# Queries and keys of heads 1 to 3 of the second layer as seven products of halves

## The chip, the cores and the metric

The kernel runs on one core of one Trainium2 chip. A core has a matrix engine (TensorE, PE in the profile), a vector engine (VectorE, DVE), a scalar engine (ScalarE, ACT), GpSimd (POOL) and SyncE (SP), which issues most of the transfers. Each engine takes its instructions strictly in the order of its own queue and waits at the head of it until the semaphores that an instruction names have been reached. Weights of PE are loaded by instructions of their own, which the profile lists as PEld. The metric is the time of one execution on the device in microseconds, the median of several executions.

## What is computed

Two pre-norm residual layers and a final norm over 512 tokens of 1024 channels, in float32. The first layer (latent attention and pooling) is not touched. The second is a retention layer of four heads. Cut to what matters:

```python
h = rms_norm(x, norm_g)
q, k, v, gate = jnp.split(h @ w_in, [1024, 2048, 4096], axis=-1)
q = apply_rope(q.reshape(B, T, 4, 256), cos_r, sin_r)
k = apply_rope(k.reshape(B, T, 4, 256), cos_r, sin_r) * 256 ** -0.5
o = retention forward + retention backward, per head   # scores q k^T times a decay, times v
o = (o - mean(o)) * rsqrt(var(o) + eps) * gn_g         # per head and token
x = x + (o * silu(gate)) @ w_out
out = rms_norm(x, final_norm_g)
```

For each head the queries and the keys are products of the 512 x 1024 activations with 1024 x 256 weights: 256 columns of queries and 256 of keys.

## The kernel before

**Split numbers.** [...] ACT casts the high part, DVE subtracts it from the source to get the low part, and a product is then three matmuls: high by high, high by low, low by high (`mm3`, lines 71 to 76). Activations are kept split in SBUF (`hT`). Weights come from DRAM into a buffer `raw` of 128 x 1024 floats (four of them), are split into `wH` (four buffers) and `wL` (three), and are used then. So every weight tile costs a load, an ACT cast of 128 x 1024 and a DVE subtraction of 128 x 1024 before the first, or the third, matmul that uses it.

**Order.** All instructions are put into the engines' queues ahead of time by a scheduling layer that follows its own costs, so the order in the queues is not that of the source; instructions under `pin` keep the program's order. The order is fixed when the program is built.

**A head of the second layer** (loop at line 983) makes its queries and keys (`qk_gemm`, `rope_pair`), then, from head 1 on, the output projection of the head before (`r_out`: 8 groups of 12 matmuls, each added into the residual by DVE, line 925), then the scores (`r_scores`), the values and gates (`vg`) and the head's output (`r_head_out`). The last 4 transposes of `r_head_out` (`turn(3)`, line 877) are kept in `pend[2]` and put behind the first group of the next head's queries. The column sums that scale the output (`out_scale`) need the squares that ACT makes of the last product, and a power on POOL (line 177).

**Queries and keys before.** Four groups per head, each 128 columns by 512 tokens, with 24 matmuls of 512 columns: 96 matmuls. Four weight tiles are loaded and split. `rope_pair` then takes two groups at a time: four multiplications of 512, one subtraction, one addition, and two splits.

**Values and gates** (`vg`, line 776) already use another scheme: tokens are halved (first and last 256), the contraction is halved (even and odd blocks of 128 channels), and the two column halves are the gates and the values. Seven products of halves then take the place of eight (the scheme of Strassen and Winograd). The sums of halves of the activations (S1 to S4) are made once per layer (`sums_of_halves`, line 704) and kept split in `forms`; those of the weights are made per head, partly by transfers that POOL issues and that add in flight (`accum_op`, line 684), partly by DVE (lines 829, 839). There the seven products run as matmuls of 512 columns. The sums of weights lie in two buffers `tw`.

Of the kernel before, what the change touches and what calls it, by code (L numbers as in the profile page):

```python
# [12 lines left out]
F32R = mybir.dt.float32r  # L13
# [3 lines left out]
ALU = mybir.AluOpType  # L17
# [20 lines left out]
def trunk(ctx: ExitStack, tc: tile.TileContext, x, positions, a_norm_g, a_w_in, a_q_norm_g, a_w_uq,  # L38
# [29 lines left out]
    def f(ap):  # L68
        return ap.bitcast(F32)
# [55 lines left out]
    fsum = C("fsum", (P, 16))  # L125
    r2, nr2, r2s = [C(n, (P, 8))[:, 0:4] for n in ("r2", "nr2", "r2s")]
    C("fill", (P, 16))
    w_in = a_w_in[0]
# [211 lines left out]
    V.tensor_reduce(out=ss, in_=ssq.rearrange("p (t q) -> p t q", q=4), axis=AX.X, op=ALU.add)  # L340
    R = C("R", (P, T))
    rp = bcast(pow_mhalf(ss, 1.0 / DM))
# [423 lines left out]
    def rope_pair(pts, tag):  # L766
# [7 lines left out]
        return split(a, tag), split(c, tag)  # L774

    def vg(h, tt=None):

# [38 lines left out]
        if tt is None:  # L816
            tt = first_sums(h)
        product("A11", "X", b11, True)
# [36 lines left out]

    def r_scores(q, k, ds, tag):
        ss = []
        for j in range(4):
            tk = slice(j * P, (j + 1) * P)
            pt = PS("sc")  # L860
            for i in range(2):
                mm3(pt, k[i][0][:, tk], k[i][1][:, tk], q[i][0], q[i][1], i == 0, i == 1)
            s = S("t")
            V.scalar_tensor_tensor(out=s, in0=pt, scalar=r2s[:, j:j + 1], in1=ds[j], op0=ALU.mult, op1=ALU.mult)
            ss.append(split(s, tag))
        return ss

    def r_head_out(ss, vv, gs, tag):


        ys = []
        sq = S("sm", (P, 4))

        def turn(t):
            pt = PS("tr")
            for m in range(4):
                nc.tensor.transpose(pt[:, m * P:(m + 1) * P], gs[t][:, m * P:(m + 1) * P], ident)
            ys.append(split(pt, tag))

        for t in range(4):  # L880
            tk = slice(t * P, (t + 1) * P)
            pt = PS("mm")
            for j in range(4):
                mm3(pt, ss[j][0][:, tk], ss[j][1][:, tk], vv[j][0], vv[j][1], j == 0, j == 3)
            V.tensor_mul(gs[t], pt, gs[t])  # L885
            act(S("t"), pt, AF.Square, scale=r2[:, t:t + 1], accum_out=sq[:, t:t + 1])
            if t:
                turn(t - 1)
        return ys, sq, lambda: turn(3)

# [92 lines left out]
    for h in range(4):  # L983
        A, B = ("qk", "y") if h % 2 == 0 else ("y", "qk")
        if h == 0:
            res = [residual(0), residual(1)]
            next(res[0])
            pq = qk_gemm(0, 1)
            sums_of_halves(0)
            sums_of_halves(1)  # L990
            next(res[0])
            pq += qk_gemm(P, 1)
            pk = qk_gemm(1024, 1)
            sums_of_halves(2)
            sums_of_halves(3)
            next(res[1])
            next(res[1])
        else:
            pq = qk_gemm(h * 256, then=pend[2])
            pk = qk_gemm(1024 + h * 256, 1)  # L1000
            rs = out_scale(pend[1])
        q = rope_pair(pq, A)
        k = rope_pair(pk + qk_gemm(1024 + h * 256 + P, 1), A)
        if h == 0:
            V.tensor_add(ss2[:, 0:4], ss2[:, 0:4], ss2[:, 4:8])
            V.tensor_copy(r2, pow_mhalf(ss2[:, 0:4], 1.0 / DM))
            V.tensor_scalar(out=nr2, in0=r2, scalar1=-1.0, scalar2=1.0, op0=ALU.mult, op1=ALU.mult)
            V.tensor_scalar(out=r2s, in0=r2, scalar1=0.0625, scalar2=1.0, op0=ALU.mult, op1=ALU.mult)
        else:
            r_out(h - 1, pend[0], rs)  # L1010
        ss = r_scores(q, k, decay(h), B)
        vv, gs = vg(h, tt0 if h == 0 else None)
        pend = r_head_out(ss, vv, gs, A)
    for i in range(2):
# [48 lines left out]
```

## Time and profile before

| | |
|---|---|
| time, three runs | 794.54, 792.81, 792.67 us; median 792.81 |
| the profiled execution | 794.41 us, of which its span of instructions is 792.6 us |
| granted TensorE clock, mean | 0.998 |
| instructions | 9592 |
| data read from HBM, written | 76.87 MB, 2.10 MB |
| transfers, mean rate | 102 GB/s |

The rows of the profile name the engine, the source line, the tile that is written and those that are read, the shape and the count, then the time in which the engine was busy and the mean duration of one. Tile names are without buffer numbers there (`mm` is any buffer of that pool in PSUM). A row of the timeline gives the start in microseconds from the span's first instruction, and the duration; successive instructions of PE and DVE overlap, so the step from start to start is what one costs in a row of them.

### The profile page before, as it was taken

How to read it: one execution, taken by the hardware profiler on the slowest of the kernel's cores; microseconds unless marked ns; L12 is line 12 of the kernel's file. 1: busy time of each engine (PE TensorE's matmuls, PEld its weight loads, DVE VectorE, ACT ScalarE, POOL GpSimd, SP SyncE). 2: the span in 40 equal slices, each digit the busy share in tenths (PEclk: the TensorE clock that was granted, in tenths of full speed). 3: DMA queues.
4: the chain of work that ended last, by engine and by line, in shares of the span. 5: the costliest groups of instructions: out<-in, count | busy, mean ns of one | idle time of the engine just before them, and what ended most of it. 6: DMA issues, size and time to landing. Idle time of an engine off the chain costs nothing. (4 is left out here: it accounts for less than half of the span.)

```text
span 792.6 us, 9592 instructions
## 1 busy us (share of the span) xinstructions
PE 781.1 (99%) x3546; PEld 642.0 (81%) x3546; DVE 579.0 (73%) x938; ACT 403.4 (51%) x670; POOL 38.6 (5%) x60
## 2 busy tenths in 40 slices
PE   9999999999999999999999999999999999999996
PEld 7888888888888888888877888888888888888885
DVE  4689986768748677899679747787377884767845
ACT  6645346666626744318654832358333583334832
POOL 0010000000000000100010100100101001010003
PEclk9999999999999999999999999999999999999999
DMA  8722233132123312353315822447324373244202
GB/s 254 226 62 83 70 82 87 39 80 91 54 72 88 103 38 69 87 152 107 107 37 133 227 56 80 111 111 210 74 79 110 103 203 84 71 122 102 85 27 108
DMA packets 87832, 80.91 MB, mean 102 GB/s; under 512 B 7868, under 2 KB 67304, under 8 KB 87784
## 3 DMA queue, kind: packets, MB, share of 16 engines
q1 hardware_dynamic: 82984, 71.11, 29.8%
q0 software_dynamic: 4352, 8.39, 7.0%
q10 hardware_dynamic: 448, 0.79, 0.3%
q8 instruction: 28, 0.46, 0.2%
q14 instruction: 20, 0.16, 0.1%
HBM read 76.87 MB, written 2.10 MB: 100 GB/s over the span
## 5 line engine op out<-in xcount | busy, mean ns | idle before, releaser
L72 PE MATMUL mm<-hT,wH 128*128 128x512 f32 x352 | 139.0, 395 | 0.3 <-ACT wH L281 0.3
L75 PE MATMUL mm<-hT,wH 128*128 128x512 f32 x352 | 137.8, 392 | 0.0
L76 PE MATMUL mm<-hT,wL 128*128 128x512 f32 x352 | 137.8, 392 | 0.0
L108 ACT CAST wH<-raw 128x1024 fp32r<-128x1024 f32 (+3 forms) x77 | 70.7, 923 | 114.4 <-PE mm L75 91.3
L109 DVE TENSOR_TENSOR wL<-raw,wH 128x1024 fp32r<-128x1024 f32 (+3 forms) x77 | 81.4, 1059 | 13.1 <-issue 4.7
L72 PEld LDWEIGHTS mm<-hT,wH 128*128 128x128 f32 x352 | 66.5, 189 | 14.0 <-ACT wH L281 0.7
L76 PEld LDWEIGHTS mm<-hT,wL 128*128 128x128 f32 x352 | 66.5, 189 | 14.0 <-DVE wL L282 0.2
L75 PEld LDWEIGHTS mm<-hT,wH 128*128 128x128 f32 x352 | 66.5, 189 | 13.6
L784 ACT CAST wH<-raw 128x1024 fp32r<-128x1024 f32 x32 | 33.7, 1054 | 50.2 <-PE mm L76 20.2
L785 DVE TENSOR_TENSOR wL<-raw,wH 128x1024 fp32r<-128x1024 f32 x32 | 38.9, 1220 | 10.4 <-issue 7.2
L784 ACT CAST wH<-tw 128x1024 fp32r<-128x1024 f32 x24 | 25.1, 1047 | 40.9 <-PE mm L76 26.3
L904 ACT ACTIVATE wH<-raw,cols 128x512 fp32r<-128x512 f32 x32 | 21.4, 717 | 43.8 <-issue 32.8
L925 DVE SCALAR_TENSOR_TENSOR xT<-mm,sm,xT 128x512 f32<-128x512 f32 (+1 forms) x33 | 24.1, 731 | 25.1 <-PE mm L76 25.0
L75 PE MATMUL mm<-y,wH 128*128 128x512 f32 x96 | 37.2, 389 | 0.0
L76 PE MATMUL mm<-y,wL 128*128 128x512 f32 x96 | 37.2, 389 | 0.0
L72 PE MATMUL mm<-y,wH 128*128 128x512 f32 x96 | 37.2, 390 | 0.0
L785 DVE TENSOR_TENSOR wL<-tw,wH 128x1024 fp32r<-128x1024 f32 x24 | 29.3, 1220 | 2.8 <-PE tr L794 1.0
L794 PE MATMUL mm<-wL,hT 128*128 128x512 f32 x80 | 31.1, 389 | 0.0
L795 PE MATMUL mm<-wH,hT 128*128 128x512 f32 x80 | 31.1, 389 | 0.0
L792 PE MATMUL mm<-wH,hT 128*128 128x512 f32 x80 | 31.0, 389 | 0.0
L885 DVE TENSOR_TENSOR l<-mm,l 128x512 f32<-128x512 f32 x16 | 11.1, 692 | 23.9 <-PE mm L76 23.9
L504 DVE TENSOR_TENSOR xT<-mm,xT 128x512 f32<-128x512 f32 x24 | 16.4, 688 | 15.0 <-PE mm L76 14.8
(361 smaller groups left out, 1903.6 us busy)
## 6 DMA issues: line engine op xcount, KB each, us to landing
raw<-in_r_w_in_dram SPq DMA_DIRECT2D x48, 512.0 KB, 3.7
raw<-in_a_w_in_dram SPq DMA_DIRECT2D x25, 512.0 KB, 4.0
raw<-in_a_w_out_dram SPq DMA_DIRECT2D x16, 512.0 KB, 3.9
raw<-in_r_w_out_dram SPq DMA_DIRECT2D x16, 512.0 KB, 5.5
tw<-in_r_w_in_dram SPq DMA_DIRECT2D x8, 512.0 KB, 3.8
tw<-in_r_w_in_dram POOLq DMA_DIRECT2D x8, 512.0 KB, 6.6
raw<-in_r_w_in_dram POOLq DMA_DIRECT2D x8, 512.0 KB, 6.0
l<-in_x_dram SPq DMA_DIRECT2D x8, 256.0 KB, 4.7
```

Source lines behind the costliest of these rows:

```text
L72: i = mm(pt, lhsT=lH, rhs=rH, start=st, stop=False)
L75: mm(pt, lhsT=lH, rhs=rL, start=False, stop=False)
L76: mm(pt, lhsT=lL, rhs=rH, start=False, stop=sp)
L108: then(nc.scalar.copy(h[:, c], raw[:, c]))
L109: then(V.tensor_sub(l[:, c], raw[:, c], f(h[:, c])))
L784: nc.scalar.copy(wh, ws[i])
L785: V.tensor_sub(wl, ws[i], f(wh))
L792: mm(o, lhsT=lh, rhs=wh[:, c], start=first and i == 0 and k2 == 0, stop=False, skip_group_check=True)
L794: mm(o, lhsT=lh, rhs=wl[:, c], start=False, stop=False, skip_group_check=True)
L795: mm(o, lhsT=ll, rhs=wh[:, c], start=False, stop=last and k2 == 1, skip_group_check=True)
L904: act(wh[:, c], raw[:, c], AF.Copy, scale=g)
L925: V.scalar_tensor_tensor(out=a, in0=pt[:, :T // n], scalar=rs[:, t:t + 1], in1=a, op0=ALU.mult, op1=ALU.add)
```

## The change

For heads 1 to 3 the queries and keys are made together by `qk_halves`. It uses the halved activations and their sums that `vg` uses; the two column halves are now the queries and the keys of the head. Of the seven products each has 24 matmuls of 256 columns (4 blocks of the contraction, 2 halves of the 128 x 256 weight columns, 3 for the split): 168 in place of 96 of 512. The seven weight operands are: the plain blocks B11 (for A11), B21 (for A12) and B22 (for S4), the sum of two blocks made by an adding transfer for S1 (`tq`, loaded ahead by `qk_load` after the `vg` of the head before, into a buffer `tw`) and for S3 (`t3`), and, for S2 and A22, the first of these sums with B22, then B21, added by DVE.

Three PSUM tiles hold the sums: X (A11, then A12, the queries of the first 256 tokens), Z (S1, then S4) and Y (S2, then S3, then A22). Since the products accumulate in place, a tile is read by DVE between two products: Z after S1 (line 839 of the changed file), Y after S2 (line 846) and after S3 (line 851). The rotation (`rope`) is done for half of the tokens at a time: per call two multiplications of 512, a subtraction and an addition of 256, and two casts and two subtractions of 256 for the split, four calls per head. The keys come out with the opposite sign, which `nr2s` undoes in the scores of heads 1 to 3. The casts and the matmuls of S1 are told to be issued after the last multiplication by the gates and the last squares of the head before (`issue_after`).

Besides: the scale `R` of the first layer moves from a buffer of its own into one of the two `x2`, the buffer `fill` is halved, the scratch memory for the transfers that POOL issues is doubled to 2048 bytes, the first matmul of each head's scores is pinned, and the adding transfers for `vg` are pinned in all heads.

```diff
--- before.py
+++ after.py
@@ -123,8 +123,8 @@
     lg = C("lg", (P, 8))
     nlb = C("nlb", (P, 8))
     fsum = C("fsum", (P, 16))
-    r2, nr2, r2s = [C(n, (P, 8))[:, 0:4] for n in ("r2", "nr2", "r2s")]
-    C("fill", (P, 16))
+    r2, nr2, r2s, nr2s = [C(n, (P, 8))[:, 0:4] for n in ("r2", "nr2", "r2s", "nr2s")]
+    C("fill", (P, 8))
     w_in = a_w_in[0]
     G.memset(mhalf, -0.5)
     vrow0 = S("t")[:8, :P]
@@ -338,7 +338,7 @@
             act(junk[:, 0:256], xt[t][q], AF.Square, accum_out=ssq[:, 4 * t + q:4 * t + q + 1])
     ss = S("sm", (P, 4))
     V.tensor_reduce(out=ss, in_=ssq.rearrange("p (t q) -> p t q", q=4), axis=AX.X, op=ALU.add)
-    R = C("R", (P, T))
+    R = S("x2")
     rp = bcast(pow_mhalf(ss, 1.0 / DM))
     nc.scalar.copy(R, rp)
 
@@ -773,6 +773,90 @@
         V.tensor_add(c, c, d)
         return split(a, tag), split(c, tag)
 
+    def qk_load(tag, h, *srcs):
+        raw = S(tag, (P, 1024))
+        v = raw.rearrange("p (a b) -> p a b", a=4)
+        for i, (r, c) in enumerate(srcs):
+            one = wv[:, r, :, c * 1024 + h * 256:c * 1024 + (h + 1) * 256]
+            if i:
+                pin(G.dma_start(v, one, accum_op=ALU.add))
+            else:
+                nc.sync.dma_start(v, one)
+        return raw
+
+    def qk_halves(h, tag, tt, then, ends):
+
+
+        ps_ = {n: PS("mm") for n in "XZY"}
+
+        def load(tag, *srcs):
+            return qk_load(tag, h, *srcs)
+
+        def product(name, a, w, first):
+            wh, wl = S("wH", (P, 1024), F32R), S("wL", (P, 1024), F32R)
+            nc.scalar.copy(wh, w)
+            V.tensor_sub(wl, w, f(wh))
+            for u in range(2):
+                o = ps_[a][:, u * H2:(u + 1) * H2]
+                for k in range(4):
+                    c = slice(k * 256 + u * P, k * 256 + (u + 1) * P)
+                    rh, rl = forms[k][name]
+                    mm(o, lhsT=wh[:, c], rhs=rh, start=first and u == 0 and k == 0, stop=False,
+                       skip_group_check=True)
+                    mm(o, lhsT=wh[:, c], rhs=rl, start=False, stop=False, skip_group_check=True)
+                    mm(o, lhsT=wl[:, c], rhs=rh, start=False, stop=k == 3, skip_group_check=True)
+
+        X, Y, Z = (ps_[n] for n in "XYZ")
+        outs = {n: [(S(tag, dt=F32R), S(tag, dt=F32R)) for _ in range(2)] for n in "qk"}
+
+        def rope(n, half, c):
+
+            ts = slice(half * H2, (half + 1) * H2)
+            v = c.rearrange("p (u t) -> p u t", u=2)
+            m1, m2 = S("t"), S("t")
+            for m, tab in ((m1, cosr), (m2, sinr)):
+                V.tensor_mul(m.rearrange("p (u t) -> p u t", u=2), v,
+                             tab[:, ts].unsqueeze(1).to_broadcast([P, 2, H2]))
+            o = S("t")
+            V.tensor_sub(o[:, :H2], m1[:, :H2], m2[:, H2:])
+            V.tensor_add(o[:, H2:], m2[:, :H2], m1[:, H2:])
+            for u in range(2):
+                hh, ll = outs[n][u]
+                us = slice(u * H2, (u + 1) * H2)
+                nc.scalar.copy(hh[:, ts], o[:, us])
+                V.tensor_sub(ll[:, ts], o[:, us], f(hh[:, ts]))
+
+        b11 = load("raw", (0, 0))
+        product("A11", "X", b11, True)
+        p1 = S("t")
+        nc.scalar.copy(p1, X)
+        then()
+        b22 = load("raw", (1, 1))
+
+        with tc.issue_after(ends[0].ins), tc.issue_after(ends[1].ins):
+            product("S1", "Z", tt, True)
+        v = S("t")
+        V.tensor_add(v, Z, p1)
+        t3 = load("raw", (0, 1), (1, 1))
+        V.tensor_add(tt, tt, b22)
+        product("S4", "Z", b22, False)
+        b21 = load("raw", (1, 0))
+        product("S2", "Y", tt, True)
+        u2 = S("t")
+        V.tensor_add(u2, Y, p1)
+        V.tensor_add(u2, Z, u2)
+        rope("k", 0, u2)
+        V.tensor_add(tt, tt, b21)
+        product("S3", "Y", t3, False)
+        V.tensor_add(v, Y, v)
+        rope("k", 1, v)
+        product("A12", "X", b21, False)
+        rope("q", 0, X)
+        product("A22", "Y", tt, False)
+        V.tensor_add(p1, Y, p1)
+        rope("q", 1, p1)
+        return outs["q"], outs["k"]
+
     def vg(h, tt=None):
 
         tags = dict(X=("mm", "mm"), Z=("mm", "tr"), Y=("mm", "sc"))
@@ -814,7 +898,7 @@
 
         b11 = [load("raw", src(0, 0, i)) for i in rng]
         if tt is None:
-            tt = first_sums(h)
+            tt = first_sums(h, pin)
         product("A11", "X", b11, True)
         p1 = [S("t") for _ in rng]
         for p in rng:
@@ -853,15 +937,15 @@
             gs[2 + p] = c
         return vv, gs
 
-    def r_scores(q, k, ds, tag):
+    def r_scores(q, k, ds, tag, rs):
         ss = []
         for j in range(4):
             tk = slice(j * P, (j + 1) * P)
             pt = PS("sc")
             for i in range(2):
-                mm3(pt, k[i][0][:, tk], k[i][1][:, tk], q[i][0], q[i][1], i == 0, i == 1)
+                mm3(pt, k[i][0][:, tk], k[i][1][:, tk], q[i][0], q[i][1], i == 0, i == 1, i == 0 and j == 0)
             s = S("t")
-            V.scalar_tensor_tensor(out=s, in0=pt, scalar=r2s[:, j:j + 1], in1=ds[j], op0=ALU.mult, op1=ALU.mult)
+            V.scalar_tensor_tensor(out=s, in0=pt, scalar=rs[:, j:j + 1], in1=ds[j], op0=ALU.mult, op1=ALU.mult)
             ss.append(split(s, tag))
         return ss
 
@@ -882,11 +966,11 @@
             pt = PS("mm")
             for j in range(4):
                 mm3(pt, ss[j][0][:, tk], ss[j][1][:, tk], vv[j][0], vv[j][1], j == 0, j == 3)
-            V.tensor_mul(gs[t], pt, gs[t])
-            act(S("t"), pt, AF.Square, scale=r2[:, t:t + 1], accum_out=sq[:, t:t + 1])
+            ends = (V.tensor_mul(gs[t], pt, gs[t]),
+                    act(S("t"), pt, AF.Square, scale=r2[:, t:t + 1], accum_out=sq[:, t:t + 1]))
             if t:
                 turn(t - 1)
-        return ys, sq, lambda: turn(3)
+        return ys, sq, lambda: turn(3), ends
 
     def out_scale(sq):
         rs = pow_mhalf(sq, 1.0 / T)
@@ -995,21 +1079,23 @@
             sums_of_halves(3)
             next(res[1])
             next(res[1])
+            q = rope_pair(pq, A)
+            k = rope_pair(pk + qk_gemm(1024 + P, 1), A)
         else:
-            pq = qk_gemm(h * 256, then=pend[2])
-            pk = qk_gemm(1024 + h * 256, 1)
             rs = out_scale(pend[1])
-        q = rope_pair(pq, A)
-        k = rope_pair(pk + qk_gemm(1024 + h * 256 + P, 1), A)
+            q, k = qk_halves(h, A, tq, pend[2], pend[3])
         if h == 0:
             V.tensor_add(ss2[:, 0:4], ss2[:, 0:4], ss2[:, 4:8])
             V.tensor_copy(r2, pow_mhalf(ss2[:, 0:4], 1.0 / DM))
             V.tensor_scalar(out=nr2, in0=r2, scalar1=-1.0, scalar2=1.0, op0=ALU.mult, op1=ALU.mult)
             V.tensor_scalar(out=r2s, in0=r2, scalar1=0.0625, scalar2=1.0, op0=ALU.mult, op1=ALU.mult)
+            V.tensor_scalar(out=nr2s, in0=r2, scalar1=-0.0625, scalar2=1.0, op0=ALU.mult, op1=ALU.mult)
         else:
             r_out(h - 1, pend[0], rs)
-        ss = r_scores(q, k, decay(h), B)
+        ss = r_scores(q, k, decay(h), B, r2s if h == 0 else nr2s)
         vv, gs = vg(h, tt0 if h == 0 else None)
+        if h < 3:
+            tq = qk_load("tw", h + 1, (0, 0), (0, 1))
         pend = r_head_out(ss, vv, gs, A)
     for i in range(2):
         gt = S("y" if A == "qk" else "qk")
```

Outside the stages of queries and keys and the first products after them, the queues of all five engines hold the same instructions in the same order as before. What the change moves shows at three places; the rows are those of head 1, and heads 2 and 3 read alike. `mm` are PSUM tiles, `wH` and `wL` the split weights.

First PE, at the end of the queries and keys and the start of the output projection of head 0. Before, where `mm_1040` is the last group of keys and `mm_1055` the first of the projection:

```order
L75 MATMUL mm_1040_4446<-hT_822_3546,wH_1038_4442 128x512
L76 MATMUL mm_1040_4446<-hT_821_3545,wL_1039_4443 128x512
L72 MATMUL mm_1055_4505<-wH_1050_4491,qk_1000_4261 128x512
L75 MATMUL mm_1055_4505<-wL_1051_4492,qk_1000_4261 128x512
L76 MATMUL mm_1055_4505<-wH_1050_4491,qk_1001_4262 128x512
L72 MATMUL mm_1055_4505<-wH_1050_4491,qk_1000_4261 128x512
```

Now, where `mm_1018` is Y with the last product, A22, and `mm_1069` to `mm_1072` are the first four groups of the projection:

```order
L806 MATMUL mm_1018_4327<-hT_823_3547,wH_1058_4565 128x256
L807 MATMUL mm_1018_4327<-hT_822_3546,wL_1059_4566 128x256
L72 MATMUL mm_1069_4621<-wH_1064_4607,qk_1002_4266 128x512
L72 MATMUL mm_1070_4635<-wH_1064_4607,qk_1007_4291 128x512
L72 MATMUL mm_1071_4649<-wH_1064_4607,qk_1012_4316 128x512
L72 MATMUL mm_1072_4663<-wH_1064_4607,qk_1032_4373 128x512
L75 MATMUL mm_1069_4621<-wL_1065_4608,qk_1002_4266 128x512
L76 MATMUL mm_1069_4621<-wH_1064_4607,qk_1003_4267 128x512
L72 MATMUL mm_1069_4621<-wH_1064_4607,qk_1002_4266 128x512
```

The first matmuls of four groups, which need high parts alone, now stand ahead of the first that needs a low part, `wL_1065`.

Then DVE, around the low parts of the projection's weights. Before (L905 makes them; L768 to L773 are the rotation, L82 the split of its results; `wL_1051` is the first weight tile of the projection):

```order
L772 TENSOR_TENSOR t_1029_4422<-t_1029_4422,t_1030_4423 128x512
L773 TENSOR_TENSOR t_1031_4424<-t_1031_4424,t_1032_4425 128x512
L905 SCALAR_TENSOR_TENSOR wL_1051_4492<-raw_1049_4489,cols_63,wH_1050_4491 128x512
L82 TENSOR_TENSOR y_1034_4433<-t_1029_4422,y_1033_4432 128x512
L905 SCALAR_TENSOR_TENSOR wL_1051_4492<-raw_1049_4489,cols_63,wH_1050_4491 128x512
L82 TENSOR_TENSOR y_1036_4437<-t_1031_4424,y_1035_4436 128x512
L768 TENSOR_TENSOR t_1041_4471<-mm_1026_4392,l1_755_3176 128x512
L769 TENSOR_TENSOR t_1043_4473<-mm_1026_4392,l1_756_3177 128x512
L905 SCALAR_TENSOR_TENSOR wL_1054_4500<-raw_1052_4497,cols_63,wH_1053_4499 128x512 x2
L770 TENSOR_TENSOR t_1042_4472<-mm_1040_4446,l1_756_3177 128x512
```

Now (L818 to L822 are the rotation, L827 the split; L989 makes the low parts, `wL_1065` is the first tile):

```order
L821 TENSOR_TENSOR t_1057_4558<-t_1055_4554,t_1056_4555 128x256
L822 TENSOR_TENSOR t_1057_4558<-t_1056_4555,t_1055_4554 128x256
L818 TENSOR_TENSOR t_1060_4594<-t_1030_4366,l1_756_3177 128x512
L827 TENSOR_TENSOR y_1020_4329<-t_1057_4558,y_1019_4328 128x256
L818 TENSOR_TENSOR t_1061_4595<-t_1030_4366,l1_757_3178 128x512
L827 TENSOR_TENSOR y_1022_4331<-t_1057_4558,y_1021_4330 128x256
L821 TENSOR_TENSOR t_1062_4598<-t_1060_4594,t_1061_4595 128x256
L822 TENSOR_TENSOR t_1062_4598<-t_1061_4595,t_1060_4594 128x256
L989 SCALAR_TENSOR_TENSOR wL_1065_4608<-raw_1063_4605,cols_63,wH_1064_4607 128x512
L827 TENSOR_TENSOR y_1020_4329<-t_1062_4598,y_1019_4328 128x256
L827 TENSOR_TENSOR y_1022_4331<-t_1062_4598,y_1021_4330 128x256
L989 SCALAR_TENSOR_TENSOR wL_1065_4608<-raw_1063_4605,cols_63,wH_1064_4607 128x512
```

The first low part of the projection stood between the two rotations before; now it stands behind all the others and nearly at the end of the last one.

Last POOL, around the power for the output's scale (L177). Before, `tw` being sums of weights for `vg` and `raw_1109` its S3 operand:

```order
L684 DMA tw_1093_4698<-in_r_w_in_dram 128x2x512
L684 DMA tw_1094_4701<-in_r_w_in_dram 128x2x512
L177 TENSOR_TENSOR sm_1028_4419<-sm_1027_4417,mhalf_61 128x4
L684 DMA raw_1109_4780<-in_r_w_in_dram 128x2x512
L684 DMA raw_1110_4783<-in_r_w_in_dram 128x2x512
```

Now, with `tw_995` the operand of S1 and `raw_1038` that of S3 of the queries and keys:

```order
L782 DMA tw_995_4225<-in_r_w_in_dram 128x4x256
L177 TENSOR_TENSOR sm_1015_4322<-sm_1014_4320,mhalf_61 128x4
L782 DMA raw_1038_4409<-in_r_w_in_dram 128x4x256
L684 DMA tw_1107_4814<-in_r_w_in_dram 128x2x512
L684 DMA tw_1108_4817<-in_r_w_in_dram 128x2x512
```

The adding transfer for S3 is issued behind the power, and the two sums for `vg` behind it.

More of the change, by code (lines that the diff above doesn't have):

```diff
@@ L1049 @@
     from concourse.bass_utils import run_bass_kernel_spmd as _run
-    nc = _bacc.Bacc("TRN2", target_bir_lowering=False, num_devices=1, dynamic_dma_scratch_size=1024)
+    nc = _bacc.Bacc("TRN2", target_bir_lowering=False, num_devices=1, dynamic_dma_scratch_size=2048)
     arrays, args = {}, []
```

## The prediction

> **What bounds the kernel now.** First the page's busy table, then PE's waits.
>
> ```profile
> PE 781.1 (99%) x3546; PEld 642.0 (81%) x3546; DVE 579.0 (73%) x938; ACT 403.4 (51%) x670; POOL 38.6 (5%) x60
> ```
>
> ```profile
> engine line waited for: us in total, times, longest us
> PE sc L160 <- POOL t L157: 1.3, 1, 1.3
> PE sc L72 <- ACT qk L81: 1.2, 1, 1.2
> ```
>
> PE is busy from end to end; its longest wait is 1.3 us. So each step that PE is spared counts in full, and each wait that it is given counts in full too, since nothing later has slack to take it back. Next the stage that is rewritten, head 2 (queries and keys, then as long a stretch of the projection), by windows (columns: busy time and count for PE, PEld, DVE, ACT, POOL, then the clock), and PE at its two ends.
>
> ```profile
> 563.08:585.45 22.37, 22.37 (x103) 18.50 (x102) 12.20 (x20) 6.98 (x12) 1.03 (x1) 1.00 0.20 64
> 585.45:607.20 21.75, 21.75 (x97) 18.02 (x96) 13.86 (x19) 5.73 (x7) 1.24 (x1) 1.00 0.35 93
> ...
> 563.08 0.48 PE L72 MATMUL mm<-hT,wH 128*128 128x512 f32 x1
> ...
> 585.22 0.39 PE L76 MATMUL mm<-hT,wL 128*128 128x512 f32 x1
> 585.45 0.39 PE L72 MATMUL mm<-wH,y 128*128 128x512 f32 x1
> 585.68 0.39 PE L75 MATMUL mm<-wL,y 128*128 128x512 f32 x1
> ```
>
> PE is full in it; DVE works 12.2 of 22.4 us. The projection's second matmul (`wL`) starts at 585.68.
>
> **What PE saves.** The price of a 256-column matmul stands at the end of this trace, where one group is cut in two.
>
> ```profile
> 782.55 0.39 PE L76 MATMUL mm<-wH,y 128*128 128x512 f32 x1
> 782.78 0.28 PE L72 MATMUL mm<-wH,y 128*128 128x256 f32 x1
> 782.89 0.28 PE L75 MATMUL mm<-wL,y 128*128 128x256 f32 x1
> ...
> 785.53 0.28 PE L76 MATMUL mm<-wH,y 128*128 128x256 f32 x1
> ```
>
> 512 columns take 0.227 from start to start, 256 take 0.120 (24 of them: 23 steps in 2.75 us), more than half. So a head pays 168 x 0.120 = 20.2 in place of 96 x 0.227 = 21.8: 1.6 us saved, 4.8 in three heads, not the eighth that seven for eight suggests. [...]
>
> **What DVE is given.** Back-to-back steps of all sizes stand in two places of the trace.
>
> ```profile
> 385.17 0.43 DVE L711 TENSOR_TENSOR t<-t,t 128x256 f32<-128x256 f32 x1 [3.60 <-ACT t L708]
> 385.51 0.42 DVE L712 TENSOR_TENSOR t<-t 128x256 f32<-128x256 f32 x1
> 385.84 0.42 DVE L713 SCALAR_TENSOR_TENSOR t<-t,t 128x256 f32<-128x256 f32 x1
> 386.18 1.22 DVE L109 TENSOR_TENSOR wL<-raw,wH 128x1024 fp32r<-128x1024 f32 x1
> 387.31 0.42 DVE L715 SCALAR_TENSOR_TENSOR t<-t,t 128x256 f32<-128x256 f32 x1
> ...
> 574.77 0.69 DVE L770 TENSOR_TENSOR t<-mm,l 128x512 f32<-128x512 f32 x1 [2.89 <-PE mm L76]
> 575.38 0.68 DVE L771 TENSOR_TENSOR t<-mm,l 128x512 f32<-128x512 f32 x1
> 575.98 0.68 DVE L772 TENSOR_TENSOR t<-t,t 128x512 f32<-128x512 f32 x1
> 576.58 0.69 DVE L773 TENSOR_TENSOR t<-t,t 128x512 f32<-128x512 f32 x1
> 577.18 0.74 DVE L905 SCALAR_TENSOR_TENSOR wL<-raw,cols,wH 128x512 fp32r<-128x512 f32 x1
> 577.84 0.69 DVE L82 TENSOR_TENSOR qk<-t,qk 128x512 fp32r<-128x512 f32 x1
> ```
>
> A step costs 0.335 us for 256 elements, 0.60 for 512, 1.13 for 1024, 0.66 for a low part of the projection. In the new order DVE has, from the first operand it splits after the output's scale (S1) up to the projection's first low part: eight of 1024 (six low parts, two sums of weights), fourteen of 512, fourteen of 256 and that low part, 0.74 to its end: 9.1 + 8.4 + 4.7 + 0.7 = **22.9 us**. When can it begin?
>
> ```profile
> 563.85 0.70 ACT L886 ACTIVATE t<-mm,r 128x512 f32<-128x512 f32 x1
> 564.66 0.17 DVE L175 TENSOR_SCALAR sm<-sm 128x4 f32<-128x4 f32 x1
> 564.92 1.03 POOL L177 TENSOR_TENSOR sm<-sm,mhalf 128x4 f32<-128x4 f32 x1 [9.07 <-DVE sm L175]
> 565.99 0.16 DVE L893 TENSOR_TENSOR sm<-sm,r 128x4 f32<-128x4 f32 x1 [1.15 <-POOL sm L177]
> ```
>
> DVE takes the scale of the head before (L893, waiting for POOL) ahead of S1, so it is free at 566.1. With no wait at all it ends at 589.0. PE's new products, packed, would end at 563.1 + 20.2 + 0.35 (the `turn` transposes) = 583.7, and four high-part matmuls later, at 584.6, PE stands before that low part. Before, the low parts were made between the two rotations, and nobody waited.
>
> **The waits inside.** I walk head 2 along the new queues, on this trace's time scale, 0.03 to 0.06 us from an end to the start that it releases. ACT prices are these; POOL's adding transfer lands 6.0 us after its issue.
>
> ```profile
> L784 ACT CAST wH<-tw 128x1024 fp32r<-128x1024 f32 x24 | 25.1, 1047 | 40.9 <-PE mm L76 26.3 <-PE tr L795 9.4 <-PE mm L75 4.8
> ...
> L684 POOL DMA_DIRECT2D raw<-in_r_w_in_dram x8 | 9.8, 1230 | 138.5 <-DVE xT L925 111.7 <-DVE qk L82 7.4 <-DVE y L82 7.2
> ...
> raw<-in_r_w_in_dram POOLq DMA_DIRECT2D x8, 512.0 KB, 6.0
> ```
>
> 1. S1's low part: 566.1 to 567.3. PE wants it at 566.8 and has it at 567.4: a wait of 0.6.
> 2. S4 follows S1 on PE with nothing between, but in the same PSUM tile Z, which DVE must read first: S1 ends at 570.2 (last start 569.9 and the 0.28 of its row), the addition ends at 570.9, S4 starts at 571.0, not 570.0: a wait of 0.9. All of PE's queue stands behind it. These two waits, 1.5 together, already take back what the products save.
> 3. S2's cast waits for the sum with B22 (to 570.2) and ends at 571.3; DVE waits 0.5 for it.
> 4. S3's operand: issued behind the power, at 566.0, landed at 572.0, cast by 573.1; DVE, which has S3 next in its queue, waits 0.6. Here the size is unknown: the pieces are 1 KB, not 2, twice as many. If bytes set the time it stays 6.0. If POOL's 1.23 us per issue doubles, it is 7.2 and the wait 1.9. If the whole transfer goes by pieces, I bound it by 10.5 (6.0 + 1.2 + another 3.3 for moving). I take the middle of the first two, 6.6.
> 5. DVE then waits 0.3 for S2's end (576.9) and 0.3 for S3's (580.7); A12's eight and sixteen matmuls, put between, cover PE there. From 580.7 DVE has eight of 512, fourteen of 256 and the low part: 4.8 + 4.7 + 0.7, which ends at **591.0** with landing at 6.0 us, 592.2 at 7.2.
> 6. The tile's second half comes two steps of 256 and one of 0.66 later, 1.4 us, when PE has three more matmuls behind it: PE goes on without stops from 592.4 (593.5) with the projection's eighth matmul. Before, that one started at 585.45 + 7 x 0.227 = 587.04.
>
> So a head comes out **5.4 to 6.5 us later**, 5.9 with 6.6 us, and three heads 17.8. Below, DVE without any wait gives 589.0 + 1.4 - 587.04 = 3.4 a head, 10 in all; above, landing at 10.5 gives about 9.5 a head, 28.
>
> **Edits taken at nothing.** `tq` is loaded when the last `vg` operand is split, near 541, lands by way of 3.8 + 6.6 us of transfers near 552, and is wanted at 564.6; without that cover the wait would be S1's. The 1.5 MB more per head meet a stage whose transfers take 0.20 of the engines. `nr2s` is one DVE operation of 0.16 once. `R`, `fill`, the scratch and the pins change no order and no wait that I can find; the sums for `vg`, now behind S3's on POOL, are wanted some 20 us after they land.
>
> **Rivals.** *PE's clock falls in the new holes.* From about 587.5 to 591 PE stands still, after 2 us in which it did four matmuls. Windows after PE's end, and matmuls ahead of the clock's rise:
>
> ```profile
> 785.90:788.70 2.80, 0.00 (x0) 0.00 (x0) 1.97 (x8) 0.18 (x1) 1.62 (x3) 1.00 0.28 109
> 788.80:792.60 3.80, 0.00 (x0) 0.00 (x0) 0.20 (x1) 0.44 (x1) 0.00 (x0) 0.50 0.49 186
> ...
> 8.40 0.63 PE L72 MATMUL mm<-hT,wH 128*128 128x512 f32 x1
> 8.82 0.63 PE L75 MATMUL mm<-hT,wH 128*128 128x512 f32 x1
> ```
>
> The granted clock was 1.00 up to 2.9 us after PE's last matmul (785.8) and 0.50 then; slow matmuls take 0.43. A hole of 3.5 us is long enough for that. If the clock takes as long to return, 2.9 us at 0.43 for 0.227 loses 1.4 a head, 4 us more in all: 815. Against it: a hole in the middle of steady work was at most 1.3 us in this trace, and shows no fall. [...]
>
> *No change.* DVE keeps up at the end (were the projection's low parts ready by 584.6, so with no more than 18.5 us of work from 566.1); then only the waits of points 1 and 2 stand against the saving: 792.8 - 3 x (1.6 - 1.5) = 792.5. Against it: 22.9 us counted.
>
> *Faster.* DVE keeps up and Z's read is hidden too: 792.8 - 4.8 = 788. It needs DVE 4.4 us shorter per head than its own steps; only PE's full row speaks for it.
>
> *Later still.* The adding transfer goes by pieces (point 4): 792.8 + 28 = 821.
>
> **How the numbers follow.** The profiled execution took 794.41 us, 1.8 more than its span of 792.6; the median of the runs is 792.81, 1.6 below it. The terms are differences on the trace and are added to the median: 792.8 + 17.8 = **810.6**, forecast **811**. Chances: forecast (DVE's queue binds, clock holds) 0.52, clock falls 0.28, later still 0.10, no change 0.05, faster 0.05. The range from 803 (DVE without waits) to 821 holds the first two, and leaves out 2 in 10 at most. Changes under 0.3% (2.4 us) can't be told from none. Faster 0.05, same 0.05, slower 0.90.
>
> **What would show it.** In the profile after: PE waiting for DVE at the projection's low part (its line 75 matmul) about 3.5 us a head, the largest wait; about 0.9 at S4 for the addition of line 839; 256-column steps of 0.120; the granted clock after those holes; the landing of POOL's transfer for S3. Wrong would be a first low part that ends before PE asks for it, or DVE steps shorter than those quoted.

## The result and the profile after

The changed kernel takes **816.77 us** (median of 5 runs, 815.22 to 818.78); the kernel before took 794.31 beside it (792.67 to 795.17). The ratio is 1.0288, interval 1.0272 to 1.0305: 22 us slower. The forecast was 811, its range 803 to 821. In the profiled execution the span grew from 792.6 to 815.0, by 22.4.

The busy table of the changed kernel, and PE's waits in it:

```profile
PE 786.4 (96%) x3762; PEld 652.4 (80%) x3762; DVE 608.5 (75%) x993; ACT 415.4 (51%) x694; POOL 46.4 (6%) x66
```

```profile
engine line waited for: us in total, times, longest us
PE mm L75 <- DVE wL L989: 10.1, 3, 3.4
PE mm L804 <- DVE t L839: 2.6, 3, 0.9
PE mm L72 <- DVE t L818: 2.3, 3, 0.8
PE mm L807 <- DVE wL L798: 1.4, 3, 0.5
```

These four are new and each comes three times, once a head. Together they are 16.4 us of standing still; all of them wait for DVE, whose share of the span is only 75%. Why an engine with a quarter of its time free makes PE wait is seen in one head. DVE in head 2 (start, duration; in brackets its own idle time and who ended it):

```profile
572.95 0.16 DVE L977 TENSOR_TENSOR sm<-sm,r 128x4 f32<-128x4 f32 x1 [1.15 <-POOL sm L177]
573.02 1.22 DVE L798 TENSOR_TENSOR wL<-tw,wH 128x1024 fp32r<-128x1024 f32 x1
...
577.23 0.69 DVE L839 TENSOR_TENSOR t<-mm,t 128x512 f32<-128x512 f32 x1
...
580.17 1.23 DVE L798 TENSOR_TENSOR wL<-raw,wH 128x1024 fp32r<-128x1024 f32 x1 [0.72 <-ACT wH L797]
...
584.08 0.69 DVE L846 TENSOR_TENSOR t<-mm,t 128x512 f32<-128x512 f32 x1 [0.41 <-PE mm L807]
...
588.01 0.69 DVE L851 TENSOR_TENSOR t<-mm,t 128x512 f32<-128x512 f32 x1 [0.17 <-PE mm L807]
...
597.60 0.75 DVE L989 SCALAR_TENSOR_TENSOR wL<-raw,cols,wH 128x512 fp32r<-128x512 f32 x1
```

From 573.02 to the projection's first low part at 597.60 DVE is idle for about 1.6 us (the brackets, and 0.3 ahead of S2's split), and from 588.01 on for nothing. The low part is not late because DVE is slow, but because it is the last of a packed queue. PE in the same head:

```profile
570.05 0.36 PE L804 MATMUL mm<-hT,wH 128*128 128x256 f32 x1
...
578.07 0.35 PE L804 MATMUL mm<-l,wH 128*128 128x256 f32 x1 [0.88 <-DVE t L839]
...
592.61 0.63 PE L72 MATMUL mm<-wH,y 128*128 128x512 f32 x2
594.02 1.01 PE L72 MATMUL mm<-wH,y 128*128 128x512 f32 x2 [0.78 <-DVE t L818]
598.41 0.80 PE L75 MATMUL mm<-wL,y 128*128 128x512 f32 x1 [3.38 <-DVE wL L989]
...
600.76 0.63 PE L72 MATMUL mm<-wH,y 128*128 128x512 f32 x1
...
603.75 0.63 PE L76 MATMUL mm<-wH,y 128*128 128x512 f32 x1
604.17 0.49 PE L72 MATMUL mm<-wH,y 128*128 128x512 f32 x1
604.50 0.40 PE L75 MATMUL mm<-wL,y 128*128 128x512 f32 x1
604.74 0.40 PE L76 MATMUL mm<-wH,y 128*128 128x512 f32 x1
```

Four matmuls of the projection, then a hole up to 598.41. And then something that the list of waits does not show: behind the hole the matmuls are slow, seven steps from 600.76 to 603.75, 0.427 each, where 0.227 is usual (604.50 to 604.74: 0.24). The windows view, cut at the places where the granted clock changes in the trace, has it in all three heads (duration, busy times, then PEclk, the granted clock):

```profile
491.73:495.14 3.41, 3.41 (x8) 2.48 (x9) 3.41 (x7) 0.00 (x0) 0.00 (x0) 0.50 0.20 57
597.54:604.36 6.82, 5.95 (x14) 4.49 (x15) 5.54 (x10) 0.59 (x2) 0.00 (x0) 0.50 0.46 143
706.77:710.18 3.41, 3.41 (x9) 2.22 (x8) 3.41 (x6) 0.00 (x0) 0.00 (x0) 0.50 0.33 101
sum 13.64, PE 12.77 PEld 9.18 DVE 12.37 ACT 0.59 POOL 0.00; mean PE 4.26 PEld 3.06 DVE 4.12 ACT 0.20 POOL 0.00
```

PE works 12.77 us at half clock. A step of 0.427 there does what one of 0.227 does at full clock, so a share of 0.200 / 0.427 = 0.468 of that time is lost: 12.77 x 0.468 = 6.0 us, an estimate that experiment 2 tests.

### The profile page after: what moved, and what is told of

Same layout as the page of the kernel before. It is cut to its first block, busy times and chain, and to the rows that moved or that the text cites. A ratio compares the mean times of both kernels' runs of the same rounds, so it can differ in the third digit from the quotient of the medians.

```text
span 815.0 us, 10145 instructions
## 1 busy us (share of the span) xinstructions
PE 786.4 (96%) x3762; PEld 652.4 (80%) x3762; DVE 608.5 (75%) x993; ACT 415.4 (51%) x694; POOL 46.4 (6%) x66
## 4 chain that ended last, share of the span: by engine, by line
PE 70%; issue 17%; DVE 8%; POOL 2%; DMA 2%; ACT 1%; SPq 0%; POOLq 0%; DVEq 0%
PE mm L75 14%; PE mm L76 14%; PE mm L72 14%; PE mm L878 3%; PE mm L879 3%; PE mm L876 3%; PE tr L575 2%; PE sc L72 2%; PE mm L804 2%; PE mm L807 2%; PE sc L76 2%; PE sc L75 2%; PE mm L806 1%; DVE t L818 1%; DMA tw<-in_r_w_in_dram 1%
## 5 line engine op out<-in xcount | busy, mean ns | idle before, releaser
L108 ACT CAST wH<-raw 128x1024 fp32r<-128x1024 f32 (+3 forms) x65 | 58.5, 901 | 114.4 <-PE mm L75 85.4
L72 PE MATMUL mm<-hT,wH 128*128 128x512 f32 x256 | 101.1, 395 | 0.7 <-ACT wH L281 0.7
L76 PE MATMUL mm<-hT,wL 128*128 128x512 f32 x256 | 100.4, 392 | 0.0
L75 PE MATMUL mm<-hT,wH 128*128 128x512 f32 x256 | 100.2, 392 | 0.0
L109 DVE TENSOR_TENSOR wL<-raw,wH 128x1024 fp32r<-128x1024 f32 (+3 forms) x65 | 66.8, 1030 | 8.0 <-PE mm L76 4.3
L72 PEld LDWEIGHTS mm<-hT,wH 128*128 128x128 f32 x256 | 48.5, 189 | 10.8 <-ACT wH L281 1.1
L76 PEld LDWEIGHTS mm<-hT,wL 128*128 128x128 f32 x256 | 48.4, 189 | 10.2
L75 PEld LDWEIGHTS mm<-hT,wH 128*128 128x128 f32 x256 | 48.5, 190 | 9.9
L75 PE MATMUL mm<-y,wH 128*128 128x512 f32 x96 | 37.2, 389 | 0.0
L72 PE MATMUL mm<-y,wH 128*128 128x512 f32 x96 | 37.2, 390 | 0.0
L75 PE MATMUL mm<-wL,qk 128*128 128x512 f32 x64 | 26.6, 416 | 6.7 <-DVE wL L989 6.7
L75 PE MATMUL mm<-wL,y 128*128 128x512 f32 (+1 forms) x68 | 27.1, 398 | 3.4 <-DVE wL L989 3.4
```

Source lines behind the costliest of these rows:

```text
L72: i = mm(pt, lhsT=lH, rhs=rH, start=st, stop=False)
L75: mm(pt, lhsT=lH, rhs=rL, start=False, stop=False)
L76: mm(pt, lhsT=lL, rhs=rH, start=False, stop=sp)
L108: then(nc.scalar.copy(h[:, c], raw[:, c]))
L109: then(V.tensor_sub(l[:, c], raw[:, c], f(h[:, c])))
```

## The experiments

Theory: DVE's order (the low part behind the products' work) costs some 16 us, and the clock that falls in the hole another 6. Rivals: the 256-column matmuls, the adding transfer, or the products' own waits cost it.

**1. The queries' rotation behind the first weights.**

```diff
-        rope("q", 0, X)
         product("A22", "Y", tt, False)
-        V.tensor_add(p1, Y, p1)
-        rope("q", 1, p1)
+        def late(ins):
+            with ExitStack() as es:
+                for i in ins:
+                    es.enter_context(tc.issue_after(i.ins))
+                rope("q", 0, X)
+                V.tensor_add(p1, Y, p1)
+                rope("q", 1, p1)
...
             us = [out_weights(h, i, hf) for i in range(2)]
+            if late and hf == 0:
+                late(us[1][2])
```

`us[1][2]` are the last two instructions that split the first half's weights.

> The queries' rotation (L818, twelve VectorE instructions, and the addition ahead of its second half) is issued only after the first half of the output projection's weights has been split; products, matmuls, transfers and buffers stay. Theory A (VectorE's order: the projection's low part of L989 stands behind some 20 us of the products' work): the low part comes 4 to 5 us sooner, TensorE's wait of 3.4 us a head at L75 and the 0.8 at L72 go, and with no hole the granted clock stays at full speed. What is left are the waits of 0.6 and 0.9 us at S1 and S4 less 1.6 us that the halved matmuls save: 793 to 798 us, at or just above the kernel before. Theory B (the matmuls of 256 columns, the transfers or the products' own waits cost the 22 us): nothing or little comes back, 808 us or more.

Measured: **794.94 us**, ratio 1.0017 (1.0007 to 1.0027). PE's waits in the second layer, all of them, and DVE's first low part:

```profile
PE mm L804 <- DVE t L839: 2.6, 3, 0.9
PE mm L807 <- DVE wL L798: 1.4, 3, 0.5
```

```profile
565.55 1.22 DVE L798 TENSOR_TENSOR wL<-tw,wH 128x1024 fp32r<-128x1024 f32 x1
...
584.46 0.74 DVE L995 SCALAR_TENSOR_TENSOR wL<-raw,cols,wH 128x512 fp32r<-128x512 f32 x1
```

From S1's split to the projection's first low part DVE now takes 18.9 us (565.55 to 584.46), where it took 24.6 (573.02 to 597.60). The instructions, matmuls and transfers are the same; thirteen DVE instructions, with the ACT copies that they feed, have another place, and with them the scheduling layer put the projection's first matmuls on PE into another order (the high-part matmuls of other groups no longer stand ahead of the first low part). 21.8 us are gone, the waits at L75 and L72 and the half clock among them (the mean clock of the run is 0.999). Theory B falls.

**2. The hole filled with matmuls.**

```diff
         product("A22", "Y", tt, False)
+        idle = PS("sc")
+        for _ in range(16):
+            fill = pin(mm(idle, lhsT=forms[0]["A11"][0][:, 0:P], rhs=hH[0], start=True, stop=True))
...
-            r_out(h - 1, pend[0], rs)
+            with tc.issue_after(fill.ins):
+                r_out(h - 1, pend[0], rs)
```

> In each head of 1 to 3, 16 matmuls of 512 columns whose result nobody reads stand behind the last product, and the projection is issued behind them; VectorE's order is the changed kernel's. They take 16 x 0.227 = 3.6 us, about as long as TensorE waits for the low part (3.4 to 3.9). If the wait itself is the whole price, nothing changes: 816 to 818 us. If the granted clock that halves behind each hole is a part of the price, TensorE keeps full speed and 1.5 to 3 us a head come back: 808 to 813 us, with no row of clock 0.5 behind the products. If the low part comes later because these matmuls keep something from VectorE, over 820.

Measured: **810.75 us**, ratio 1.0214 (1.0196 to 1.0233). The waits, and windows around the three places:

```profile
PE mm L75 <- DVE wL L992: 3.2, 3, 1.1
PE mm L804 <- DVE t L839: 2.6, 3, 0.9
```

```profile
488.00:500.00 12.00, 10.93 (x49) 8.66 (x48) 9.49 (x19) 1.48 (x4) 0.00 (x0) 1.00 0.52 150
594.00:606.00 12.00, 10.93 (x48) 8.68 (x47) 9.31 (x18) 0.87 (x4) 0.00 (x0) 1.00 0.49 146
700.00:712.00 12.00, 10.93 (x49) 8.63 (x48) 9.30 (x17) 1.64 (x3) 0.00 (x0) 1.00 0.44 136
```

The extra matmuls do nothing useful and end no wait: DVE's order is the changed kernel's, the low part still sets when PE goes on, and 1.1 us of the hole are left. But the clock stays at 1.00, and the kernel is **6.0 us faster** (816.77 to 810.75; the spans differ by 6.1, 815.0 to 808.9). That is the price of the clock by itself. What is left, 810.75 - 793.16 = 17.6 us by the medians and 808.9 - 792.6 = 16.3 by the spans, is what the change costs with the clock held. Of the 17.6, experiment 1 takes back 15.8 (810.75 to 794.94): that is the price of DVE's order. The other 1.8 stay with the new order too.

**3. The kernel before with 256-column matmuls.** `gemm_T` runs its eight k twice, once for each half of the columns, for the 12 queries' and keys' products of heads 1 to 3.

```diff
-            for k in range(8):
-                mm3(pt, uH[:, k], uL[:, k], hH[k], hL[k], k == 0, k == 7)
+            n = T // cuts
+            for c in range(cuts):
+                for k in range(8):
+                    ...
```

> The kernel before, with the queries' and keys' products of heads 1 to 3 cut into two halves of 256 columns (the same three products with the same weights, each weight tile loaded twice): 288 matmuls of 0.227 us become 576. By the 0.120 us of a 256-column matmul in the values' products that is 288 x (2 x 0.120 - 0.2267) = +3.8 us: 796 to 798 us. If two halves cost no more than a whole (0.1135 each), 793. If the weights' load cannot be hidden behind 256 columns here, over 800.

Measured: 797.36 us, ratio 1.0054 (1.0035 to 1.0074), so +4.2 us (2.8 to 5.9) where 3.8 were worked out. One row of its PE and another 20 steps on:

```profile
465.92 0.28 PE L330 MATMUL mm<-hT,wL 128*128 128x256 f32 x1
...
468.31 0.28 PE L329 MATMUL mm<-hT,wH 128*128 128x256 f32 x1
```

2.39 us for 20 steps: 0.120, as the prediction took it. By this price the 168 matmuls of a head save 1.6 us, not an eighth.

**4. The adding transfer ahead of the power.** `rs = out_scale(pend[1])` moves from ahead of `qk_halves` to behind it.

> The output scale's power on GpSimd is issued behind the products, so that GpSimd hands out the adding transfer of S3's weights without waiting for the squares of the head before; VectorE's order is unchanged. If that transfer is on the path (it landed some 6.2 us after issue, and VectorE's split of S3's weights waited for it), the low part comes 0.5 to 1.5 us sooner in each head: 812 to 815 us, less if the shorter hole spares the clock. If VectorE is bound by its own work or by the products ahead of S3, no change: 816 to 818.

Measured: 816.67 us, ratio 1.029 (1.0269 to 1.0311): no change. GpSimd's issue, and DVE's split of S3's weights and the next instruction that waits:

```profile
562.02 1.30 POOL L782 DMA_DIRECT2D raw<-in_r_w_in_dram  x1 [7.09 <-issue]
```

```profile
579.34 1.22 DVE L798 TENSOR_TENSOR wL<-raw,wH 128x1024 fp32r<-128x1024 f32 x1
...
584.07 0.69 DVE L846 TENSOR_TENSOR t<-mm,t 128x512 f32<-128x512 f32 x1 [1.25 <-PE mm L807]
```

The transfer is issued 10.9 us sooner (562.02, before it 572.88), and the split of S3 starts 0.83 sooner, without a wait. But the next instruction, L846, starts at 584.07 as it did at 584.08: its wait for S2's end on PE has grown from 0.41 to 1.25. The queues of PE, ACT and DVE hold the same order as in the changed kernel, and the time is the same: the landing was not on the path, and the 0.72 and the 0.41 were one wait in two pieces.

**5 to 7. The waits that experiment 1 has left.** A version without them should beat both kernels. Three edits on experiment 1's kernel: A12 to between S1 and S4; the output scale behind S1's split; both.

```diff
         t3 = load("raw", (0, 1), (1, 1))
+        b21 = load("raw", (1, 0))
+        product("A12", "X", b21, False)
```

```diff
-            product("S1", "Z", tt, True)
+            low = product("S1", "Z", tt, True)
+        with tc.issue_after(low.ins):
+            rs = out_scale(sq)
```

`low` is the instruction that makes S1's low part.

> The kernel of the first experiment (queries' rotation behind the projection's first weights), with the product A12 moved from behind S3 to between S1 and S4, and its operand's load with it: TensorE then has 24 matmuls x 0.120 = 2.9 us of work while VectorE adds on Z. If the 0.9 us at S4 are a price of their own, they go in each head: 794.9 - 3 x 1.03 = 791 to 792.5 us. If TensorE only waits later (for S2's or S4's low part, or at the projection), no change: 794 to 796.

> The kernel of the first experiment, with the output scale (L175, the power on GpSimd, the product with r2) issued behind the split of S1's weights, so that VectorE no longer waits 1.15 us for GpSimd ahead of S1's low part. If S1's wait of 0.5 us (0.63 a head from start to start) comes from there, 794.9 - 3 x 0.63 = 793 us. If S1's low part is bound by the rounded copy on ScalarE or by the order behind the last gates, no change: 794.5 to 796.

> The kernel of the first experiment with both edits: A12 between S1 and S4, and the output scale behind S1's split. With no wait left in the products the fewer matmuls should show: 1.6 us a head by the step of 0.120, so 793.2 - 4.8 = 788.4, and up to 791 with the 0.4 us a head that the first experiment has left unexplained. If the waits only move to the scores or to the projection, 794 or more.

All three missed: 796.58 (1.0033, 1.002 to 1.0046), **810.84** (1.0217, 1.0194 to 1.0239), **806.81** (1.0162, 1.0141 to 1.0182). The waits of A12 early:

```profile
PE mm L804 <- DVE t L847: 1.7, 3, 0.6
PE mm L807 <- DVE wL L798: 1.4, 3, 0.5
```

S4's wait is gone, and S3 has one: it waits for DVE's reading of Y after S2 (L847 in this file), which a part of A12 had covered. Two gaps have one cover. Why this run is 1.6 us slower than experiment 1, with about as much waiting in its list, wasn't measured by itself. The scale behind S1's split, on POOL and on ACT in head 2:

```profile
571.64 1.93 POOL L177 TENSOR_TENSOR sm<-sm,mhalf 128x4 f32<-128x4 f32 x1 [19.21 <-DVE sm L175]
573.55 1.33 POOL L782 DMA_DIRECT2D raw<-in_r_w_in_dram  x1
574.35 1.76 POOL L684 DMA_DIRECT2D tw<-in_r_w_in_dram  x1
```

```profile
581.34 1.99 ACT L797 CAST wH<-raw 128x1024 fp32r<-128x1024 f32 x2 [5.36 <-DMA raw<-in_r_w_in_dram]
```

The power comes later on POOL, and the adding transfer of S3's weights stands behind it. It is issued at 573.55 and lands at 581.26, 7.7 us later; ACT, and behind it DVE and PE, wait for it. In head 2 the clock is 0.50 from 585.5 to 588.9. Here the transfer is the bound that it was not in experiment 4. Experiment 7 has the same order on POOL, and ACT waits 3.9 us for the transfer in head 2. PE's longest wait is another there, 2.4 us a head at most, at a matmul of the projection that the scheduling layer had put ahead of S3; how much of its loss is the transfer's was not tried.

**8 to 10. S2 as the cover, and the transfer ahead of the power.** S2 writes Y and needs nothing of Z, so it can stand between S1 and S4; S4 then stands between S2 and S3, A12 between S3 and A22. In the second edit `out_scale` comes behind the load of S3's weights in the code.

```diff
-        product("S4", "Z", b22, False)
-        b21 = load("raw", (1, 0))
         product("S2", "Y", tt, True)
+        product("S4", "Z", b22, False)
+        b21 = load("raw", (1, 0))
...
         t3 = load("raw", (0, 1), (1, 1))
+        with tc.issue_after(low.ins):
+            rs = out_scale(sq)
```

> The kernel of the first experiment with S2 in front of S4: S2 (on Y) covers VectorE's addition on Z, S4 (on Z) its addition on Y, and A12 stays between S3 and A22. The run with A12 moved has shown that A12 covers a wait of its own (for L847, 0.6 us) where it stands. If the waits of the products are what is left over the saving, only S1's 0.63 us a head stays: 794.9 - 3 x 1.03 = 791.8, up to 793 if S2's operand (the sum on tw, then ScalarE's copy and the low part) comes a little late. If the wait moves once more, 794 to 797.

> The run with the output scale behind S1's split once more, but with GpSimd's adding transfer of S3's weights handed out ahead of the power, as in the kernel of the fourth experiment. If the 15 us that the other order lost are the transfer's (it was issued some 1.7 us later and landed 7.8 us after), they come back whole, and S1's wait is the rest: 792.5 to 793.5. If it is the scale behind the split that costs, by another way than the transfer, 800 or more.

> Both: S2 in front of S4, the output scale behind S1's split, the adding transfer ahead of the power. No wait of over 0.3 us should stay in the products; 1.6 us a head of the fewer matmuls are left: 788.5 to 791 us, faster than both kernels. If S2's operand is late by what S1 gains, 791 to 793.

Measured: 794.17 (0.9993, 0.998 to 1.0007), 796.18 (1.0023, 1.0012 to 1.0033), and **792.31** (0.9973, 0.9959 to 0.9986). PE's longest waits in the products, of the three in this order:

```profile
PE mm L807 <- DVE wL L798: 2.8, 6, 0.5
```

```profile
PE mm L804 <- DVE t L840: 3.7, 3, 1.2
```

```profile
PE mm L807 <- DVE wL L798: 1.4, 3, 0.5
```

Experiment 9 gives 14.7 of the 15.9 us that experiment 6 had lost against experiment 1 back (810.84 to 796.18). Between the two only the order on POOL differs, so they were the transfer's, with the half clock that followed from it. S1's wait is off the list, but S4's has grown from 0.9 to 1.2, since PE comes to it sooner and DVE does not: nothing is gained, and the time is a miss too (792.5 to 793.5 were expected). In experiment 8 S4's wait is gone and S2's low part waits 0.5 in its place. Its 794.17 is what had been expected if the wait moved once more. Only with both is one wait of 0.5 a head left. This version comes out 0.27% below the kernel before by the ratio, 2.1 us, and 1.2 us below it by the medians (792.31 and 793.48). The interval lies below 1, but the difference is under the 0.3% below which, by the prediction, a change can't be told from none (the 25 runs of the kernel before beside it lie between 792.56 and 797.01): level with the kernel before, or just ahead of it.

**11. The last wait.** On the kernel of experiment 10, the transposes of the head before (`then`) and the scale are issued behind S2's split.

> The run with all waits covered, in which S2's low part is still 0.63 us a head late, with the last transposes of the head before, their split and the output scale behind S2's split on VectorE. If the 0.63 comes from those three instructions ahead of S2's low part, it goes: 792.3 - 3 x 0.63 = 790.4 us, in all some 3 us under the kernel before. If S2's low part is bound by the sum on tw and ScalarE's copy of it, no change: 792 to 793.

Measured: 795.27 us, ratio 1.0017 (1.0005 to 1.003). A miss; PE's waits, and DVE at S2's split:

```profile
PE mm L807 <- DVE wL L798: 2.5, 6, 0.5
```

```profile
569.14 1.22 DVE L798 TENSOR_TENSOR wL<-tw,wH 128x1024 fp32r<-128x1024 f32 x1 [1.11 <-ACT wH L797]
```

DVE reaches S2's split sooner and idles 1.11 us there for ACT's copy, which follows DVE's own sum: the three instructions had stood in a gap. Put behind it, they make the next low part late: six waits in place of three.

## Why the prediction was right, and where not

To compare, 6.97 us are taken off the times of the changed kernel's head 2, whose first product starts at 570.05; the prediction set it at 563.08.

- **DVE's queue binds, and where** (22.9 us of work from 566.1 up to the low part): right. DVE begins at 566.05 and the low part ends at 591.38, forecast 591.0 to 592.2; of these 25.3 us 1.6 are waits, so the work took 23.7, 0.8 more than counted. The hole was forecast from 587.5 to 591 and is there up to 591.44. Experiment 1 shows the cause: with the order changed and the work kept, it is gone.
- **Point 1, S1's low part, 0.6:** 0.47 by the list of waits.
- **Point 2, S4 behind the addition on Z, 0.9, start at 571.0:** 0.88, start at 571.10.
- **Point 3, S2's cast, 0.5:** 0.31.
- **Point 4, the adding transfer:** 6.6 us were taken between 6.0 and 7.2. It was issued at 572.88 and landed at 579.02, 6.14 us later; the page's median for this row is 6.2. Before, with 256 pieces of 2 KB, it was 6.0; 512 pieces of 1 KB took 0.1 to 0.2 us more. The bound of 10.5 by pieces had 3.3 us for moving that no row of the prediction shows (an estimate from the page of the kernel before comes to it: 4352 packets of POOL's queue took 7.0% of the time of 16 engines in 792.6 us, 0.204 us each, and 256 more of them, over 16 engines, take 3.3); nothing like it came. DVE's wait was 0.72, and experiment 4 shows that at this size it costs nothing, for point 5 takes it over. That was not said in the prediction.
- **Point 5, 0.3 and 0.3:** 0.41 and 0.17.
- **Point 6, 5.4 to 6.5 us a head:** with the clock held by experiment 2, 16.3 / 3 = 5.4 by the spans and 17.6 / 3 = 5.9 by the medians, against 5.4 for a landing of 6.0 us and 5.9 as forecast. The sum of 17.8 holds to 0.2 us by the medians and 1.5 by the spans.
- **PE's saving, 0.120 a step:** right (experiment 3: 20 steps in 2.39 us, and +4.2 us where 3.8 were worked out).
- **Not named:** the 0.78 at L818, where the projection's third group waits for a PSUM tile that the rotation still has to read. It lies inside the same hole, and went with it.

**The step that failed** is the choice of the likeliest case, "DVE's queue binds, clock holds", 0.52. The first half held; the clock fell, in all three holes, as the rival of 0.28 had it. That rival was mis-sized too: 1.4 us a head, 2.0 measured (experiment 2). It took the length of the slow stretch from the fall at the program's end, 2.9 us after PE's last matmul. The steps of 3.41 us in the changed kernel's trace (last section) give that another reading: in the kernel before the clock was full from 10.51 to 788.74, which is 228 x 3.413, and the last of these steps, 785.33 to 788.74, still had 0.48 us of matmuls in it, so the 2.9 us are what was left of it. So 811 became 816.8: of the 23.6 us between the medians (816.77 - 793.16), 17.6 stay with the clock held, 17.8 forecast, and 6.0 are the clock's, which the likeliest case put at nothing. The range, up to 821, holds the measured time because it was drawn to hold this rival as well.

The rival *no change* was right about its condition: once the low part is in time (experiment 1), the waits of points 1 and 2 take back what the products save. It put the rest at -0.1 us a head; the medians have +0.6, the spans +0.3. Steps of 0.19 to 0.23 us where a new operand begins (the row at 578.07 and the next at 578.26), in place of 0.120, are a part of that; the rest wasn't measured by itself.

## What to carry to other kernels

When work moves from an engine that is full to one that is 75% busy, count the second engine's queue from the last point where it can start up to the first result that the full engine asks for; a mean share says nothing about that stretch. A product that only waits for an evacuation needs another one, on another PSUM tile, in front of it: count the gaps and the covers, for moving one cover only moved the wait here (0.9 us at S4 gone, 0.6 at S3 new in experiment 5; 0.5 at S2 new in experiment 8). And a hole in PE's work can cost more than its own length: here the granted clock was 0.50 for 3.41 to 6.82 us behind holes of 3.4 us, and it fell to 0.50 in experiments 6 and 7 as well, where no wait was over 2.4 us.

## What the runs showed of the hardware that was not expected

**The half clock came in whole steps.** The three stretches are 3.41, 6.82 and 3.41 us long, and lie on one grid: (706.77 - 491.73) / 63 = 3.413, and 491.73 + 31 x 3.413 = 597.54. Between them the clock is full for 102.4 us each time (495.14 to 597.54, 604.36 to 706.77), 30 x 3.413. The trace also shows what went with the length: in head 2 the step that began at 597.54 still had 0.87 us of the hole in it (PE goes on at 598.41), and the clock came back only after the next one, which had 3.41 us of matmuls. In heads 1 and 3 the steps from 491.73 and from 706.77 had 3.41 us of matmuls at once, and the clock was back after them. The trace of experiment 4 has the same: behind first slow steps with 0.79 and 2.87 us of matmuls in them a second one followed, behind the one with 3.28 none.

**The clock fell behind steps that were not empty.** It fell in all three holes. In heads 1 and 3 the step ahead of the fall had 0.08 and 0.40 us of matmuls in it (488.31 to 491.73, 703.35 to 706.77); in head 2 (594.13 to 597.54) it had the two matmuls of 594.02, 0.87 us of work. Other runs go further. In experiment 4 the clock fell at 488.61, only 0.7 us into head 1's hole, behind a step with 1.85 us of matmuls. In experiment 6 no single wait was over 2.1 us and in experiment 7 none over 2.4, and the clock fell in all three heads of both; the steps ahead had 0.50 to 1.73 us of matmuls in them:

```profile
582.08:585.50 3.42, 0.50 (x2) 0.30 (x2) 3.08 (x3) 1.86 (x3) 0.00 (x0) 1.00 0.68 138
585.50:588.91 3.41, 2.94 (x13) 2.94 (x14) 3.38 (x6) 1.67 (x3) 0.00 (x0) 0.50 0.75 254
```

These two rows are head 2 of experiment 6. Where 1.1 us of the hole were left (experiment 2, steps with 2.34 us of matmuls) the clock stayed at 1.00 in all three heads. So in these runs it did not go by the length of a hole alone: it fell 0.7 us into one, and 2.9 us after the last matmul of the kernel before. Nor did it go by the matmuls in one step alone: near the end of experiment 6 a step with 1.58 us of them (800.53 to 803.95) is followed by one at full clock. What decides was not tried further.

**An adding transfer's landing time moved.** S3's took 6.14 us in the changed kernel and 7.7 in experiment 6, with the same bytes and pieces. In both another one is issued 0.8 us behind it; what differs is that the core's transfers moved 143 GB/s in that stretch in place of 108, and that the load of the projection's weights begins 1.4 us behind the transfer's issue in place of 4.3. That the load is the cause was not tried by itself.
